# A hybrid encoder layer on one core: another model decides the order of each engine's instructions

## The chip, the core and the metric

The kernel runs on one core of one Trainium2 chip. A core has five engines that each take their own queue of instructions in order: TensorE (PE, with its weight loads shown apart as PEld), VectorE (DVE), ScalarE (ACT), GpSimd (POOL) and SyncE (SP). In this kernel SP issues all transfers between device memory (DRAM) and the on-chip memory (SBUF). Matmul results stand in PSUM, which DVE and ACT read. Engines wait for each other on semaphores. The metric is device time in microseconds (us); each figure is a median of several executions, and one execution more is taken with the profiler.

## The reference

One layer of a bidirectional encoder with parallel head groups, applied with the same weights to two requests: 1024 rows (x_sample) and 256 rows (x_prompt) of width 2048. Each has 256 rows of memory.

```python
hn = rms_norm(x, norm_g)
proj = hn @ w_in
xbc, z_ssd, dt_raw, q, k, v, z_att, mq, z_mem = split_cols(proj, IN_SIZES)
xbc = silu(centred_dwconv(xbc, conv_w, conv_b))           # 5 taps over the rows
y = ssd_scan(forward) + ssd_scan(backward) + d_skip * xs  # chunks of 128 rows, 16 heads
o_ssd = rms_norm(y * silu(z_ssd))                          # two groups of 512
o_att = window_attention(q, k, v, sink) * silu(z_att)      # |t-s| <= 128, 8 heads, 2 kv heads
o_mem = softmax(mq @ mk.T) @ mv * silu(z_mem)              # 4 heads over 256 memory rows
return x + concatenate([o_ssd, o_att, o_mem]) @ w_out
```

All values are float32. q, k, mq and mk are normalised per head.

## The kernel before

The 1280 rows are ten tiles of 128 rows, eight of the sample and two of the prompt, in two row groups of five tiles. A large product with weights is computed in 16 steps over the contraction. Each float32 operand is split into a rounded part (h, or xH) and a rest (l, or xL), and each product is three matmuls: h with xH, l with xH, h with xL (L269 to L271 in `block_tok`, L304 to L306 in `block_feat`). Per step SP loads a weight tile (wraw, L228 or L286), ACT makes wh (L219, or L222 with a gain), DVE makes wl (L220 or L223), and PE multiplies it with all five row tiles. These are the main matmuls. Their results stand in five PSUM banks (acc), which an evacuation function empties.

Beside this main stream runs the side work, written as Python generators that are stepped between the main steps: normalisation statistics, window attention (`attn`, L558), memory attention (`mem_attn`, L665) and the two passes of the SSD scan (`ssd_up`, L757, `ssd_down`, L877). `run` (L942) asks for so many side steps per main step; the rates are written by hand. So the order in which the Python program emits instructions is fixed by hand. It isn't the order on the chip: on leaving the context (L1159), the library's scheduler simulates the machine and picks, for each engine, the next instruction by emission order and by readiness in its simulation; `high_priority` (L253, L273) shifts some of them forward. Buffers are handed out in the same pass, from rings of a fixed size. The queues that result are static: on the chip each engine takes its queue in that order.

The steps of memory attention for one row tile, `mem_attn`, are: SP loads the queries (mq, L669); ACT squares them, DVE sums (mss, L673), POOL makes the reciprocal root (mr, L133 and L134), DVE scales (L677); PE transposes them (pmq, L683); ACT and DVE split them (mqh L685, mql L687); PE makes the scores of two pairs of heads (pms, L699 to L701); DVE takes the maximum (mm, L703), ACT the exponential (mpr, L708), DVE the reciprocal of the sum (mden, L710) and the scaling (L713); PE transposes the probabilities (pmt, L721), ACT copies them (mpT, L723), PE multiplies them with the values (pmo, L734), DVE with the gate (moT, L737); SP stores the transposed result to DRAM (oT, L750).

The output product, four blocks of 512 columns for each row group (`w_out_rows`), takes its stationary operand from four quads xH0 to xH3 (with xL0 to xL3), of which there is one buffer each. While the last block of one group runs, `refill_o` (L975) refills each quad for the other group as soon as the block is past it. Quads 0 and 1 (window and memory attention) are loaded already transposed, by `fill_direct`: load chd (L207), xH on ACT (L210), xL on DVE (L211). Quads 2 and 3 (SSD) are loaded by rows, by `fill_transposed`: load ch (L191), scale on DVE (L193), transpose on PE (pr, L196), xH on ACT (L199), xL on DVE (L200). The evacuation `ev_out` (L392) loads the rows of x (yt, L400), adds the PSUM bank on DVE (L401) and stores (L402). chd, ch and the yt of tiles 0 and 3 share one ring of three buffers (tag "ch", CH in L29).

The context is opened in `kernel`, which the diff touches.

## Time and profile before

| | us |
|---|---|
| median of 3 runs | 1927.21 |
| lowest and highest run | 1923.53 and 1927.83 |
| the profiled execution | 1923.56 |
| its span on the core | 1921.8 |
| PE busy | 1878.3 |
| DVE busy | 1050.8 |
| ACT busy | 763.8 |
| POOL busy | 136.2 |
| mean granted TensorE clock | 0.994 |

The profile's page gives busy time per engine, then the span cut into 40 equal slices with the busy share of each in tenths. Matmuls are pipelined and their ends are modelled, so a busy PE can still be short of its best rate. A row of waits reads: the engine, tile and line that waited, the engine, tile and line that ended the wait, the total in us, how often, the longest. A row of groups reads: line, engine, operation, what it writes and reads, the shape and count, then busy time and the mean of one in ns, then idle time before it and what ended that. A row of the queue of SP or of a timeline reads: start, duration, engine, line, operation. Rows of transfers end with the median time in us from issue to landing. A row of a stretch reads: from and to, length, busy time and count of PE, PEld, DVE, ACT and POOL, the granted clock of TensorE (1 is full), the share of the transfer engines that is busy, and GB/s.

### The profile page before, as it was taken

To read this page: it belongs to the slowest core of one execution; us is meant where nothing else is said; L and a number is where in the kernel's file an instruction comes from. 1 tells how busy PE (TensorE), PEld (TensorE's weight loads), DVE (VectorE), ACT (ScalarE), POOL (GpSimd) and SP (SyncE) were. 2 spreads that over 40 slices of the span, in tenths; PEclk is the share of its full clock that TensorE was granted. 3 is DMA by queue.
4 is the path that set the end of the run, shared out by engine and by line. 5 is a ranking of instruction groups with operands and counts; after the bars stand their busy time and mean duration, and the time that the engine had idled before them with its cause. 6 is when DMAs were issued, how large, how long until landed. Compare 5 with 4: busy or idle time off the path is not lost.

```text
span 1921.8 us, 28750 instructions
## 1 busy us (share of the span) xinstructions
PE 1878.3 (98%) x10568; PEld 1636.4 (85%) x10568; DVE 1050.8 (55%) x2097; ACT 763.8 (40%) x1720; POOL 136.2 (7%) x183
## 2 busy tenths in 40 slices
PE   7999999999999999999999999999999999999999
PEld 6798899998898879899977777988987778878887
DVE  4455327586564554876676555574775554442222
ACT  6556423242442545532325445333633433321111
POOL 0111000000010000100110110100010000000000
PEclk9999999999999999999999999999999999999999
DMA  8766533323443455543435567763465344554442
GB/s 269 264 201 186 165 104 95 107 92 109 122 123 118 159 161 154 155 123 94 118 110 158 147 182 250 233 189 116 151 197 180 118 133 133 179 175 132 134 120 70
DMA packets 191341, 289.42 MB, mean 151 GB/s; under 512 B 18976, under 2 KB 68192, under 8 KB 191200
## 3 DMA queue, kind: packets, MB, share of 16 engines
q1 hardware_dynamic: 191200, 287.58, 48.7%
q8 instruction: 83, 1.36, 0.3%
q14 instruction: 58, 0.48, 0.1%
HBM read 230.59 MB, written 56.92 MB: 150 GB/s over the span
## 4 chain that ended last, share of the span: by engine, by line
PE 80%; DMA 10%; DVE 4%; ACT 4%; issue 2%; POOL 1%; SPq 0%; ACTq 0%; DVEq 0%; POOLq 0%
PE acc L269 14%; PE acc L271 14%; PE acc L270 14%; PE acc L304 9%; PE acc L306 9%; PE acc L305 9%; DMA rf<-ac 2%; PE po L647 1%; DMA rb<-ac 1%; PE py L860 1%; DMA chd<-in_mem_turned_dram 1%; PE ppt L636 1%; PE pmo L734 1%; DMA xst<-in_x_sample_dram 1%; PE psc L606 1%
## 5 line engine op out<-in xcount | busy, mean ns | idle before, releaser
L269 PE MATMUL acc<-wh,xH 128*128 128x512 f32 (+1 forms) x1568 | 619.2, 395 | 15.6 <-ACT wh L219 13.7
L270 PE MATMUL acc<-wl,xH 128*128 128x512 f32 (+1 forms) x1568 | 602.7, 384 | 2.5 <-DVE wl L220 2.5
L271 PE MATMUL acc<-wh,xL 128*128 128x512 f32 (+1 forms) x1568 | 602.6, 384 | 0.0
L220 DVE TENSOR_TENSOR wl<-wraw,wh 128x512 fp32r<-128x512 f32 (+1 forms) x416 | 282.3, 680 | 393.8 <-ACT wh L219 383.7
L219 ACT ACTIVATE wh<-wraw 128x512 fp32r<-128x512 f32 (+1 forms) x416 | 254.4, 613 | 557.8 <-PE acc L271 249.5
L304 PE MATMUL acc<-xH,wh 128*128 128x320 f32 x1280 | 405.9, 317 | 0.4 <-DVE zs L331 0.4
L306 PE MATMUL acc<-xH,wl 128*128 128x320 f32 x1280 | 397.8, 311 | 0.0
L305 PE MATMUL acc<-xL,wh 128*128 128x320 f32 x1280 | 396.3, 310 | 0.0
L269 PEld LDWEIGHTS acc<-wh,xH 128*128 128x128 f32 x1568 | 297.3, 190 | 77.9 <-ACT wh L219 15.2
L270 PEld LDWEIGHTS acc<-wl,xH 128*128 128x128 f32 x1568 | 297.5, 190 | 61.3 <-issue 5.0
L271 PEld LDWEIGHTS acc<-wh,xL 128*128 128x128 f32 x1568 | 297.1, 189 | 57.2 <-issue 1.4
L304 PEld LDWEIGHTS acc<-xH,wh 128*128 128x128 f32 x1280 | 241.1, 188 | 6.4 <-issue 4.9
L305 PEld LDWEIGHTS acc<-xL,wh 128*128 128x128 f32 x1280 | 241.0, 188 | 3.2 <-issue 3.1
L306 PEld LDWEIGHTS acc<-xH,wl 128*128 128x128 f32 x1280 | 240.9, 188 | 0.9 <-issue 0.9
L223 DVE SCALAR_TENSOR_TENSOR wl<-wraw,vec,wh 128x512 fp32r<-128x512 f32 x64 | 48.0, 751 | 120.8 <-ACT wh L222 120.8
L222 ACT ACTIVATE wh<-wraw,vec 128x512 fp32r<-128x512 f32 x64 | 46.3, 724 | 137.5 <-PE acc L271 135.4
L379 DVE SCALAR_TENSOR_TENSOR c<-u,vec,c 128x638 f32<-128x638 f32 (+1 forms) x96 | 84.9, 884 | 1.0
L850 ACT ACTIVATE rb<-rb,wj_all 128x128 f32<-128x128 f32 x160 | 52.2, 390 | 46.6 <-DMA rb<-ac 46.5
L621 ACT ACTIVATE lg<-lg,nm 128x384 f32<-128x384 f32 (+1 forms) x80 | 45.1, 564 | 47.5 <-DVE nm L615 45.5
L850 ACT ACTIVATE rf<-rf,wj_all 128x128 f32<-128x128 f32 x160 | 53.3, 391 | 23.6 <-DMA rf<-ac 23.6
L803 POOL TENSOR_TENSOR ya<-xs,dco 128x512 f32<-128x512 f32 x20 | 29.4, 1479 | 401.7 <-DVE dco L788 259.8
L214 DVE SCALAR_TENSOR_TENSOR xL<-chd,vec,xH 128x640 fp32r<-128x640 f32 (+1 forms) x48 | 40.6, 859 | 29.3 <-ACT xH L213 28.6
(236 smaller groups left out, 1771.5 us busy)
## 6 DMA issues: line engine op xcount, KB each, us to landing
wraw<-in_w_in_laid_dram SPq DMA_DIRECT2D x288, 256.0 KB, 2.8
wraw<-in_w_out_laid_dram SPq DMA_DIRECT2D x128, 256.0 KB, 2.7
chd<-in_x_turned_dram SPq DMA_DIRECT2D x32, 320.0 KB, 3.8
rf<-ac SPq DMA_DIRECT2D x40, 256.0 KB, 3.8
rb<-ac SPq DMA_DIRECT2D x40, 256.0 KB, 4.0
out_dram<-yt SPq DMA_DIRECT2D x40, 256.0 KB, 3.2
wraw<-in_w_mem_laid_dram SPq DMA_DIRECT2D x32, 256.0 KB, 4.9
xst<-in_x_sample_dram SPq DMA_DIRECT2D x32, 256.0 KB, 4.4
```

The costliest lines, as they stand in the source:

```text
L219: A.activation(h, raw, AF.Copy)
L220: V.tensor_sub(l, raw, h.bitcast(F32))
L222: A.activation(h, raw, AF.Copy, scale=g)
L223: V.scalar_tensor_tensor(out=l, in0=raw, scalar=g, in1=h.bitcast(F32), op0=ALU.mult, op1=ALU.subtract)
L269: T.matmul(ps[t][:, :n], sh, h[:, :n], start=(k_ == 0), stop=False)
L270: T.matmul(ps[t][:, :n], sh, l[:, :n], start=False, stop=False)
L271: T.matmul(ps[t][:, :n], sl, h[:, :n], start=False, stop=(k_ == KT - 1))
L304: T.matmul(o, sh, cur["H", q][:, m, c], start=(k == 0), stop=False)
L305: T.matmul(o, sh, cur["L", q][:, m, c], start=False, stop=False)
L306: T.matmul(o, sl, cur["H", q][:, m, c], start=False, stop=(k == KT - 1))
L379: V.scalar_tensor_tensor(out=c[:, :n], in0=u[:, k:k + n], scalar=cw[k], in1=c[:, :n], op0=ALU.mult, op1=ALU.add)
L850: A.activation(r[:, c], r[:, c], AF.Identity, bias=wj_all[:, t, h:h + 1])
```

## The change

One argument of the context is set. With it the scheduler takes the times by which it orders instructions from the library's timeline simulator in place of its default model. The Python program that emits instructions, the tiles, the rings and their sizes, and the stages are unchanged.

```diff
-    with _tile.TileContext(nc) as tc:
+    with _tile.TileContext(nc, schedule_with_timeline_sim=True) as tc:
         hymba_encoder_kernel(tc, *args)
```

Both programs hold the same instructions: 10,020 matmuls, 2,097 on DVE, 1,523 on ACT, 179 on POOL and 1,130 transfers on SP. Set side by side, 4,902 of the matmuls, 1,565 of the DVE instructions, 1,101 of those on ACT, 718 of the transfers and 22 on POOL have another place in their queue. Half of the DVE, ACT and SP instructions move by two places or fewer. On PE the largest move is 294 places. Around the refill of the last output blocks the queue of PE reads as follows after the change (line, tile written and tiles read, shape, count):

```
L269 Matmult acc_17113<-wh_17192,xH0_16731 128x512
...
L683 Matmult pmq_16595<-ident_84,mq_16559 128x128 x4
L699 Matmult pms_16607<-mkH_113,mqh_16600 128x256
...
L721 Matmult pmt_16662<-ident_84,mpr_16617 128x128 x4
L721 Matmult pmt_16669<-ident_84,mpr_16655 128x128 x4
L734 Matmult pmo_16697<-mpT_16667,mv_115 128x128 x4
L734 Matmult pmo_16703<-mpT_16674,mv_115 128x128 x4
L196 Matmult pr_16940<-ident_84,ch_16937 128x128 x4
L196 Matmult pr_16950<-ident_84,ch_16947 128x128 x4
L196 Matmult pr_16981<-ident_84,ch_16978 128x128 x4
L196 Matmult pr_16991<-ident_84,ch_16988 128x128 x4
L196 Matmult pr_17022<-ident_84,ch_17019 128x128 x4
L269 Matmult acc_17116<-wh_17120,xH0_16731 128x512
```

In the queue before, 30 main matmuls stand between pmq_16595 and the last pmo_16703, and 225 between that and the last refill transpose, pr_17183; after the change these are 0 and 48.

## The prediction

> **What bounds the kernel now.** I read the page's busy table, its slices and chain, then the waits of PE over the whole span and by stretch, then the stretch from 1600 us. TensorE is the bound: PE is busy in every slice, and the chain is 80% PE.

> ```profile
> span 1921.8 us, 28750 instructions
> PE 1878.3 (98%) x10568; PEld 1636.4 (85%) x10568; DVE 1050.8 (55%) x2097; ACT 763.8 (40%) x1720; POOL 136.2 (7%) x183
> PE   7999999999999999999999999999999999999999
> PE 80%; DMA 10%; DVE 4%; ACT 4%; issue 2%; POOL 1%; SPq 0%; ACTq 0%; DVEq 0%; POOLq 0%
> ```

> So only two things can change: how long PE waits, and at what clock it runs. The matmuls are the same, with the same shapes. The waits of PE, whole span (all rows sum to some 39 us, of which 7.9 is the wait before the first matmul):

> ```profile
> PE acc L269 <- ACT wh L219: 13.7, 4, 7.9
> PE psc L606 <- ACT pT L637: 3.7, 3, 1.8
> PE pr L196 <- DVE ch L193: 3.4, 4, 1.6
> PE pyb L903 <- DVE state L912: 3.0, 1, 3.0
> PE acc L270 <- DVE wl L220: 2.5, 5, 1.4
> PE py L860 <- DVE rb L853: 2.3, 3, 1.3
> ```

> Cut by stretch, the waits sum to 10 us from the first matmul to 210 us, 19.5 us in 23 waits between 210 and 1600, and one wait of 1.6 us after 1600. The last matters most: between 1600 and 1720 the kernel finishes the last attention tiles of the second row group and refills the stationary operand for the last four output blocks, and PE loses 1.6 us over it. The queue shows why: the loads that refill are spread over 50 us, beside main matmuls.

> ```profile
> 1626.49 1.06 SPq L669 DMA_DIRECT2D mq<-mq  x1
> 1650.09 0.94 SPq L750 DMA_DIRECT2D oT<-moT  x1
> 1655.79 1.06 SPq L207 DMA_DIRECT2D chd<-oT  x2
> 1669.45 1.06 SPq L191 DMA_DIRECT2D ch<-o  x2
> 1699.97 0.36 SPq L191 DMA_DIRECT2D ch<-o  x1
> ```

> (mq starts the last memory-attention tile, oT stores its result, chd and ch are refill loads.) The profiled execution took 1923.56 us: 1921.8 of span and 1.8 around it. It equals the fastest of the three runs (1923.53) and is 3.65 under their median; my sum is made against 1923.56.

> **The change part by part.** No instruction is added or removed; every engine's queue is re-sorted. I place each PE instruction of the new order at the sum of the time that the instructions ahead of it took on PE in the profile.

> *Side work sinks behind the main matmuls.* In the new order attention, SSD and memory attention stand later, the main matmuls earlier. The query transposes pmq (L683) of the five memory-attention tiles of the second group move later by 21, 36, 48, 60 and 58 us of PE work. The main matmuls ahead of them cost the same 0.227 us, so this is free until main matmuls run out. They run out at the last tile: between its first transpose and its last pmo matmul (L734) stood 30 main matmuls, now none; between its first transpose and the eighth of the ten refill transposes pr (L196) stood 240, which are 54 us, now 23, which are 5.2 us. PE takes its queue in order, so behind pmq it can do nothing else.

> *What the chain there needs.* SP has the same inversion: the load of mq (L669), formerly 18 rows ahead of oT's store, now stands 3 ahead of it, and then come all four chd loads, five ch loads, two yt loads, one more ch load, two stores and two ch loads, with no weight load between. chd, ch and two of five yt tiles share one ring of three buffers (CH, L29). Durations are means or medians of the profile's groups:

> ```profile
> mq<-mq SPq DMA_DIRECT2D x10, 256.0 KB, 3.6
> oT<-moT SPq DMA_DIRECT2D x10, 256.0 KB, 3.3
> chd<-oT SPq DMA_DIRECT2D x16, 320.0 KB, 3.7
> ch<-o SPq DMA_DIRECT2D x20, 256.0 KB, 3.2
> yt<-in_x_sample_dram SPq DMA_DIRECT2D x32, 256.0 KB, 4.4
> out_dram<-yt SPq DMA_DIRECT2D x40, 256.0 KB, 3.2
> ```

> 1. mq load 3.6, square 0.63, sum 0.69, rsqrt on POOL 0.19 and 1.01, scaling 0.69, with hand-overs: 6.9 us.
> 2. pmq to the last pmo: transposes 0.6, split 0.58 and 0.68, twelve pms 1.4, maximum 0.69 and 0.17, two exp with their accumulator reads 1.3, reciprocal 0.17, two scalings 0.7, pmt 0.6, copy 0.59, pmo 1.8: 9 us.
> 3. Two moT products 0.8, store 3.3, chd load 3.7, split 0.73 and 0.82, which together with one more split (0.8) frees a ring buffer; ch load 3.2, scaling 0.48: 13.8 us.
> 4. pr 0.3; the third ch load waits for the fourth chd, itself late in the ring: 3.0; two more pr and their scalings 0.6: 3.9 us.
> 5. yt load into the buffer that a pr frees, 4.4, and the addition (L401) 0.69, without which PE's next main matmul has no PSUM bank: 5.1 us.
> 6. yt store 3.2, ch load 3.2, scaling 0.48, a little queueing, and behind it on DVE the wl split 0.69 of the next weights: 7.9 us.

> That is 46.6 us. PE has work in it: 2.3 us between mq's issue and pmq, 23 main matmuls 5.2, and side matmuls (4 pmq, 12 pms, 8 pmt, 8 pmo, 32 pr) 8.0: 15.5 us. PE waits 46.6 - 15.5 = 31.1 us. With the slower landings that such loads also had here (the chain lists a ch load of 4.80 us) it is 37.5; with the quick ones (some 2.6 us for a ch load) 27. I take 34, between median and slow. The old wait of 1.6 goes.

> *The clock.* After PE's wait of 2.44 us before 199.2, its granted clock was 0.50 for 5.4 us, and matmuls stood 0.43 us apart instead of 0.227:

> ```profile
> 199.20:204.60 5.40, 5.38 (x12) 4.02 (x13) 1.38 (x2) 3.79 (x9) 0.00 (x0) 0.50 0.38 120
> ```

> The new chain has waits of about 4, 14, 4, 4 and 2.5 us, so its own matmuls run at half clock (pms, pmt and pmo on the path: +2.6), and the first 12 main matmuls behind it (12 x 0.2 = 2.4): +5. Bounds: 0 if the clock stays up, 8 if all 13 us of PE work doubled and lay half on the path. [...]

> *The waits elsewhere.* All 23 waits between 210 and 1600 stand at side matmuls or evacuations that the new order puts later, each by more PE work than it waited (the 3.0 at pyb by 6.8 us, the 1.8 at psc by 4.8). But their inputs come from ACT and DVE queues that were re-sorted too, and steps that wait for each other still follow each other (pyf behind the cb copy, pst behind xf). Bounds: 0 and -19.5; I take -8, nearer to none than to all, as a wait put later often comes back one step on. Before 210 us the transfers are the limit (DMA share 0.71, against 0.47 after), and only the order of splits changes: 0 to -10, I take -3. With those go one or two slow-clock stretches: -1. Together -12.

> Sum: 1923.6 - 1.6 + 34 + 5 - 12 = 1949.

> **The rivals.** (a) *Nothing comes back elsewhere*: the waits removed are replaced, one for one. For it: ACT and DVE carry the same chains. Against: PE has more main work ahead of every old wait. Time: 1949 + 12 = 1961, up to 1966 with slow landings. (b) *The order pays elsewhere and ends faster*: all 29.5 us of old waits go, with 4 to 5 us of low clock, -34 in all, and the refill chain costs less than that. For it: 23 of 23 places have more cover. It decides for faster from a refill below 34 us with its clock, that is, ch and chd loads at their quick 2.6 us while the weight loads are out of their way: 1923.6 - 1.6 + 27 + 2 - 34 = 1917. Against: these loads took up to 4.8 us here. (c) *The refill chain is cheap but the rest goes as I forecast*: 1923.6 - 1.6 + 27 + 2 - 15 = 1936. (d) *The new order says nothing on the chip, because waits decide the sequence anyway*: 1924; against it, queues are taken in order, and 217 main matmuls have left the gap.

> **How the numbers follow.** Forecast 0.68 (1938 to 1960: refill 31 to 38, clock 2 to 7, elsewhere -17 to -8), (a) 0.15, (c) 0.10, (b) 0.05, (d) 0.02. A measurement of this kernel tells 0.2% (3.9 us) from no change. Slower by more: forecast, (a) and (c), 0.93. The range reaches to (c) and most of (a): 1934 to 1965.

> **What would show it.** PE idle 30 to 38 us in one cluster near 1680 to 1740, at pmq, pmt, pr and L269, the largest a pr that waits 13 to 16 us for L193; ch and chd landings packed into 35 us with hardly a weight load; granted clock near 0.5 there; PE waits between 210 and 1600 near 11 us. Wrong if the pr wait is under 8 us, or if main matmuls wait for wh or wl all along, which the same order could bring if ACT is late.

## The result, and the profile after

| | before | after |
|---|---|---|
| median of 4 runs, us | 1926.41 | 1946.60 |
| lowest and highest run | 1923.53 and 1927.83 | 1945.28 and 1951.25 |
| the profiled execution | 1923.56 | 1947.09 |
| its span | 1921.8 | 1945.4 |

The changed kernel takes 1.0112 times as long, 95% interval 1.0095 to 1.0128. The forecast was 1949, range 1934 to 1965. The page of the profile after, its first lines, the slices of PE and of its clock, and the shares of the chain:

```profile
span 1945.4 us, 28765 instructions
PE 1880.3 (97%) x10568; PEld 1639.4 (84%) x10568; DVE 1049.7 (54%) x2097; ACT 761.6 (39%) x1720; POOL 136.3 (7%) x183
...
PE   7999999999999999999999999999999999869999
...
PEclk9999999999999999999999999999999999879999
...
PE 77%; DMA 14%; ACT 3%; DVE 3%; issue 1%; SPq 1%; POOL 0%; POOLq 0%; ACTq 0%; DVEq 0%
```

PE is busy 2.0 us longer and idle 21.6 us longer (span less busy: 43.5, now 65.1). Where before every slice but the first read 9, the two from 1653 to 1751 us now read 8 and 6, and the granted clock dips to 8 and 7 tenths in the same two. The waits of PE from 1680 to 1740 us in the kernel after (us in total, times, longest):

```profile
PE pr L196 <- DVE ch L193: 16.8, 3, 12.2
PE pmq L683 <- DVE mq L677: 3.7, 1, 3.7
PE pmt L721 <- DVE mpr L713: 1.9, 1, 1.9
PE acc L269 <- DVE yt L401: 1.8, 1, 1.8
PE pms L699 <- ACT mqh L685: 0.7, 1, 0.7
```

These are 24.9 us where the kernel before lost 1.6. They are waits of the chain that the prediction walked, sorted here by size; in time, pmq comes first, then pms, pmt, pr, the acc that waits for yt, and a last pr. The queue of SP after, from mq on (start, duration, engine, line, operation):

```profile
1683.26 0.33 SPq L400 DMA_DIRECT2D yt<-in_x_prompt_dram  x1
1683.64 0.42 SPq L669 DMA_DIRECT2D mq<-mq  x1
...
1702.40 0.51 SPq L750 DMA_DIRECT2D oT<-moT  x1
1705.01 4.94 SPq L207 DMA_DIRECT2D chd<-oT  x4
1710.41 6.31 SPq L191 DMA_DIRECT2D ch<-o  x5
1719.24 1.33 SPq L400 DMA_DIRECT2D yt<-in_x_sample_dram  x2
1721.15 0.33 SPq L191 DMA_DIRECT2D ch<-o  x1
...
1727.17 0.89 SPq L191 DMA_DIRECT2D ch<-o  x2
1731.69 0.33 SPq L228 DMA_DIRECT2D wraw<-in_w_out_laid_dram  x1
```

No weight load is issued between 1684 and 1731. The loads of oT and o, which before lay over 50 us beside main matmuls, follow each other here, and no main matmul runs between 1686.9 and 1722.9. The chain that ended last passes through the same steps (start, duration, piece):

```profile
1683.64 3.41 DMA mq<-mq
...
1699.30 2.62 PE pmo L734 x16
...
1702.40 2.54 DMA oT<-moT
...
1705.40 3.38 DMA chd<-oT
...
1710.41 3.01 DMA ch<-o
...
1719.24 2.82 DMA yt<-in_x_sample_dram
...
1722.87 4.24 DMA out_dram<-yt
1727.17 2.60 DMA ch<-o
...
1730.49 0.63 PE pr L196 x4
```

Not all of the loss is waiting. I take the time from the start of each PE instruction to the start of the next, without the waits, and subtract the median of its kind (same line and shape; these medians add up to 1851 us in both programs). Between 1600 and 1760 us this excess is 1.6 us before and 9.7 after, and it grows where the granted clock is low: 8.4 of the 9.7 belong to matmuls that started while it was 0.50. So the refill costs 23.3 us of waits and 8.1 of slow matmuls, 31.4 together. The whole span grew by 23.6: the rest of the kernel became 7.8 us shorter. 6.2 of these lie between 180 and 210 us (waits and excess: 7.3 before, 1.1 after), 1.6 in all the rest. That last figure is a balance of larger ones, and two traces of the changed kernel show how far one trace carries: from 210 to 1600 us its waits and excess are 32.7 us here and 20.8 in x11 below, with 33.3 before.

### The profile page after: what moved, and what is told of

The parts are those of the page before. It is cut to its first block, busy times and chain, and to the rows that moved or that the text cites. A ratio compares the mean times of both kernels' runs of the same rounds, so it can differ in the third digit from the quotient of the medians.

```text
span 1945.4 us, 28765 instructions
## 1 busy us (share of the span) xinstructions
PE 1880.3 (97%) x10568; PEld 1639.4 (84%) x10568; DVE 1049.7 (54%) x2097; ACT 761.6 (39%) x1720; POOL 136.3 (7%) x183
## 4 chain that ended last, share of the span: by engine, by line
PE 77%; DMA 14%; ACT 3%; DVE 3%; issue 1%; SPq 1%; POOL 0%; POOLq 0%; ACTq 0%; DVEq 0%
PE acc L270 13%; PE acc L269 13%; PE acc L271 13%; PE acc L304 9%; PE acc L306 9%; PE acc L305 9%; DMA rb<-ac 2%; DMA rf<-ac 2%; DMA xst<-in_x_sample_dram 2%; PE po L647 2%; PE ppt L636 1%; PE py L860 1%; DMA chd<-in_mem_turned_dram 1%; ACT rf L850 1%; PE pmo L734 1%
## 5 line engine op out<-in xcount | busy, mean ns | idle before, releaser
L270 PE MATMUL acc<-wl,xH 128*128 128x512 f32 (+1 forms) x1568 | 602.0, 385 | 3.9 <-DVE wl L220 3.8
L269 PE MATMUL acc<-wh,xH 128*128 128x512 f32 (+1 forms) x1568 | 584.1, 392 | 19.2 <-ACT wh L219 16.4
L220 DVE TENSOR_TENSOR wl<-wraw,wh 128x512 fp32r<-128x512 f32 (+1 forms) x416 | 284.7, 688 | 338.1 <-ACT wh L219 329.1
L219 ACT ACTIVATE wh<-wraw 128x512 fp32r<-128x512 f32 (+1 forms) x416 | 253.5, 612 | 491.0 <-PE acc L271 213.4
L304 PE MATMUL acc<-xH,wh 128*128 128x320 f32 x1280 | 401.4, 314 | 0.8 <-ACT qs L340 0.6
L269 PEld LDWEIGHTS acc<-wh,xH 128*128 128x128 f32 x1568 | 293.5, 189 | 82.6 <-ACT wh L219 20.2
L270 PEld LDWEIGHTS acc<-wl,xH 128*128 128x128 f32 x1568 | 296.2, 189 | 63.2 <-DVE wl L220 6.5
L851 DVE COPY_PREDICATED rb<-upper,rf 128x512 f32<-128x512 uint32 x40 | 31.5, 788 | 70.2 <-ACT rb L850 62.5
## 6 DMA issues: line engine op xcount, KB each, us to landing
wraw<-in_w_in_laid_dram SPq DMA_DIRECT2D x288, 256.0 KB, 2.8
wraw<-in_w_out_laid_dram SPq DMA_DIRECT2D x128, 256.0 KB, 2.7
rf<-ac SPq DMA_DIRECT2D x40, 256.0 KB, 3.5
rb<-ac SPq DMA_DIRECT2D x40, 256.0 KB, 4.8
out_dram<-yt SPq DMA_DIRECT2D x40, 256.0 KB, 2.7
wraw<-in_w_mem_laid_dram SPq DMA_DIRECT2D x32, 256.0 KB, 4.9
xst<-in_x_sample_dram SPq DMA_DIRECT2D x32, 256.0 KB, 4.5
```

The costliest lines, as they stand in the source:

```text
L219: A.activation(h, raw, AF.Copy)
L220: V.tensor_sub(l, raw, h.bitcast(F32))
L269: T.matmul(ps[t][:, :n], sh, h[:, :n], start=(k_ == 0), stop=False)
L270: T.matmul(ps[t][:, :n], sh, l[:, :n], start=False, stop=False)
L304: T.matmul(o, sh, cur["H", q][:, m, c], start=(k == 0), stop=False)
```

## The experiments

Each group of runs had its own runs of the kernel before beside it (medians 1926.4 for the result, 1922.0 for x1 to x4, 1921.3 for x5 to x8, 1919.9 for x9 to x11), so I compare ratios. "Refill" is the stretch from 1600 to 1760 us.

| run | ratio to before, 95% interval | waits at the refill | excess there | lost 180 to 210 |
|---|---|---|---|---|
| before | 1 | 1.6 | 1.6 | 7.3 |
| after | 1.0112 (1.0095 to 1.0128) | 24.9 | 9.7 | 1.1 |
| x1 default order, 'o' 1.6 | 1.0117 (1.0099 to 1.0135) | 19.6 | 9.7 | 8.1 |
| x2 default order, 'o' 2.0 | 1.0032 (1.0015 to 1.0048) | 7.7 | 6.0 | 6.8 |
| x3 new order, early attention | 0.9960 (0.9946 to 0.9975) | 1.3 | 0.7 | 0.7 |
| x4 new order, no round trip | 1.0035 (1.0023 to 1.0047) | 11.1 | 7.8 | 1.0 |
| x5 early block, default | 1.0093 (1.0078 to 1.0108) | 1.4 | 2.2 | 2.4 |
| x6 early block, timeline | 1.0088 (1.0071 to 1.0105) | 1.4 | 2.3 | 0.1 |
| x7 new order, memory last | 1.0050 (1.0032 to 1.0068) | 12.9 | 11.4 | 1.0 |
| x8 x3 and x7 together | 0.9966 (0.9952 to 0.9980) | 1.1 | 1.1 | 0.2 |
| x9 default order, early attention | 0.9982 (0.9969 to 0.9994) | 0.8 | 0.5 | 6.5 |
| x10 as x3 | 0.9966 (0.9952 to 0.9980) | 0.7 | 0.5 | 1.5 |
| x11 after again | 1.0080 (1.0059 to 1.0101) | 21.9 | 9.4 | 0.1 |

### x1 and x2: the same loss under the default order

My theory is that the loss is one place, the refill that no main matmul covers, because memory attention ends too late. The rival is that the simulator's order costs a little everywhere. If the theory is right, the default order must lose the same when memory attention is made late by hand, and lose in steps with the cover.

```diff
-          'o': 2.6})
+          'o': 1.6})
```

> The kernel before (default model), with one number changed: the side steps asked for per main step of the output blocks fall from 2.6 to 1.6 (RATES 'o'). That alone puts the memory attention of the second row group as late as the new order put it: in the queue of PE 7,611 main matmuls stand ahead of the last pmo and of the first five refill transposes, as in the changed kernel (before: 7,389 and 7,524 to 7,554). Theory (the loss is the refill that no main matmul covers): the same group of waits appears, a pr wait of 11 to 15 us for L193 first, 20 to 27 us of PE waits in all near 1690 to 1735, and some 8 us of slow matmuls beside them; 1926 + 23 + 6 = 1955 us, between 1945 and 1962. Rival (the simulator's order costs it, by many places all over): the default order is kept, so 1926 us, within 5.

The other run has 2.0 in that place.

> The same edit by half: 'o' from 2.6 to 2.0. 7,519 main matmuls stand ahead of the last pmo, 92 fewer than in the changed kernel, and 7,575 to 7,591 ahead of the first five refill transposes. Theory: 92 main matmuls are 21 us of cover, about what the chain from the last pmo to the last pr needs beyond its own work, so most of the loss is not there yet: 1927 to 1937 us, best guess 1932 (waits of 1 to 3 us at two or three refill transposes). Rival: 1926 us.

Measured: x1 1943.97 beside 1921.98, x2 1928.58. PE's waits of x1 from 1600 to 1760 us:

```profile
PE pr L196 <- DVE ch L193: 14.9, 5, 12.5
PE pmq L683 <- issue: 3.1, 3, 1.4
PE acc L269 <- DVE yt L401: 0.9, 1, 0.9
PE pmt L721 <- DVE mpr L713: 0.7, 2, 0.5
```

and of x2:

```profile
PE pmq L683 <- issue: 4.7, 3, 2.2
PE pr L196 <- DVE ch L193: 2.7, 4, 1.0
PE acc L269 <- DVE yt L401: 0.3, 1, 0.3
```

The default order, with one rate lowered, waits at four of the same five places, with much the same longest wait (12.5, against 12.2), and loses 22 us. The rival's 1926 is out. With 92 main matmuls (21 us) of cover the long pr wait is gone, and 6 to 7 us are lost, as expected. In size x1 is a miss: I expected 29 us more than before, and it was 22 (1943.97 is just under the range of 1945 to 1962; the kernel before ran 4 us faster beside it than in the result). The waits came to 19.6 us, under the 20 to 27 expected. By the two traces waits and excess at the refill grew by 26.1 us, so the rest of the gap lies outside it, where single traces of one kernel differ by as much.

### x3: the new order with the cover restored

```diff
-... 'mq': 2.75, 'zm': 2.54,
+... 'mq': 4.0, 'zm': 5.2,
```

> The changed kernel (timeline simulator), with two numbers changed: the side steps asked for beside the blocks mq and zm of the second row group rise from 2.75 and 2.54 to 4.0 and 5.2. Window attention of that group ends earlier, memory attention starts earlier, and 7,473 main matmuls stand ahead of the last pmo in place of 7,611, 7,541 ahead of the first refill transpose. Theory: of the 24.9 us of waits at the refill some 3 stay, and the slow clock there goes (8 us): 1946.6 - 22 - 8 = 1917 us, with about 4 us of new waits at the earlier window attention 1921; range 1914 to 1930. Rival (the order costs everywhere): nothing of this touches the rest, 1940 to 1947 us.

Measured: 1914.32 beside 1921.98. All waits of PE from 1600 to 1760 us in x3:

```profile
PE pr L196 <- DVE ch L193: 1.3, 2, 1.1
```

The order of the simulator stays, the refill is covered, and the kernel is now faster than both others. So the order itself costs nothing on balance; what it does to one place does (what the two rates do by themselves is x9's question). The rival (1940 to 1947) is out.

### x4: what part the round trip through oT has

```diff
-                return [part(fill_direct, q, j, oT_d[q][grp][:, j, :]) for j in range(4)]
+                return [part(fill_direct, q, j, oT_d[q][0][:, j, :]) for j in range(4)]
```

> The changed kernel, but the last refill of the quad of memory attention reads oT of the first row group, which has long been stored, in place of the second group's (so the memory part of the last five row tiles is left out of the output product). All transfers, matmuls and the order of PE at the refill stay; only the wait of the four chd loads for the last oT store goes. Theory (the chain pmo, store of oT, chd, ch, pr is what PE waits for): the 12.2 us wait at pr falls below 3, PE waits near the refill 5 to 8 us in place of 24.9, and 1946.6 - 18 - 4 = 1924 us, range 1919 to 1931. Rival (the ring of three buffers and the packed transfers are the limit, whatever oT does): the pr wait stays above 8 us, 1938 us or more.

Measured: 1929.30 beside 1921.98, with the memory part of the last five row tiles left out of the output. PE's waits of x4 from 1600 to 1760 us, but for one of 0.7:

```profile
PE pr L196 <- DVE ch L193: 5.5, 3, 2.4
PE pmq L683 <- issue: 3.0, 1, 3.0
PE pmt L721 <- DVE mpr L713: 1.9, 1, 1.9
```

The 12.2 is gone, as the theory says; the rival's 8 us or more at pr isn't there. By the ratios (1.0112 to 1.0035) some 15 us go, where I had expected 22: of the waits 11.1 stay, not 5 to 8, and of the excess 7.8 of 9.7, not half. The several waits of 1 to 3 us that are left go with a low clock as well: 0.50 from 1686 to 1696 and from 1703 to 1709, with PE 73% and 86% busy.

### x7 and x8: the memory quad last

```diff
-            need((attn, mem_attn, ssd_down, ssd_down)[q], range(grp * 5, grp * 5 + 5))
-            if q < 2:
-                return [part(fill_direct, q, j, oT_d[q][grp][:, j, :]) for j in range(4)]
+            need((attn, ssd_down, ssd_down, mem_attn)[q], range(grp * 5, grp * 5 + 5))
+            if q in (0, 3):
+                return [part(fill_direct, q, j, oT_d[q // 3][grp][:, j, :]) for j in range(4)]
...
-    inputs['w_out_laid'] = _np.concatenate([att, w[1536:], w[:1024]]) ...
+    inputs['w_out_laid'] = _np.concatenate([att, w[:1024], w[1536:]]) ...
```

> The changed kernel with the order of the quads in the output product changed: window attention, SSD, SSD, memory attention, in place of attention, memory, SSD, SSD (the rows of w_out are laid out to match). Memory attention's quad is then refilled last and needed last, 180 main matmuls (41 us) into the next block. The lateness of memory attention itself stays: 7,611 main matmuls stand ahead of its last pmo. Theory (the long wait is the round trip through oT standing ahead of the refill transposes in the queues): pmq and pmt still wait 3.7 and 1.9 us, the 12.2 at pr falls to waits of 2 to 3 each; some 11 us of waits in place of 24.9 and half of the slow matmuls: 18 us under the changed kernel, 4 us over the kernel before (1926 beside 1922; range 1920 to 1932). Rival (packed loads and the ring of three set the refill's pace, whatever comes first): no less than 14 us over the kernel before.

> The timeline simulator's order with both repairs: the side rates beside mq and zm of the second row group at 4.0 and 5.2, and the memory quad last. Theory: no wait at the refill (1.3 with the rates alone), a 3.5 us wait of a transpose of the window attention gone; so 2 to 3 us under the version with the rates alone, 10 us under the kernel before (1912 beside 1922; range 1908 to 1917). Rival: the refill has no more to give, 1914 within 2.

Measured: x7 1931.55 beside 1921.34, x8 1914.68. x7 takes the long wait away with nothing left out of the computation (the waits at pr are now five, 6.1 us in all, 2.5 the longest), so it was the round trip standing ahead of the refill transposes. But it is 10 us over the kernel before, where I had said 4: the excess didn't halve, it was 11.4. x8 gives nothing over x3: where the refill is covered, the order of the quads has no more to save, which is what its rival said.

### x5 and x6: the early part alone, without a verdict

The new order's own gain lies near 200 us. To test it alone, the part up to `gate_att(0)` is put into a block with its own order (the body moves in by four columns; later x_stats loads no longer wait for a load in the block).

```diff
+    with tc.block(schedule_with_timeline_sim=True):
+        vec = const([P, R_N], "vec")
...
+        gate_att(0)
+    last_load[0] = None
     queue(0, attn, range(4))
```

The control has `tc.block()`.

> A control for the next one. The kernel before, with everything up to the end of gate_att(0) (the first 240 us or so) put into a block of its own, ordered by the default model. The boundary costs something by itself, because no load crosses it: worked from the rows of before, one wait of some 22 us at the first matmul behind it. So 1922 + 22 = 1944 us, between 1936 and 1956. The place at 195 to 205 us stays as in the kernel before: an L269 that waits 2.4 to 2.8 us for wh and matmuls at half clock behind it, some 7 us lost in waits and slow matmuls between 180 and 210 us.

> The same block, ordered by the timeline simulator; everything behind it is ordered by the default model, as in the control. Theory (of the 9 us that the new order gains away from the refill, 6 come from this one place near 200 us, where the default order puts a weight load behind two loads of x rows that wait for a buffer): 6 us under the control, the 2.4 us wait and the half clock gone, about 1 us lost between 180 and 210 us. Rival (the gain is spread over the waits between 210 and 1600 us, as I had forecast): within 2 us of the control.

Measured: x5 1940.14, x6 1940.86, beside 1921.34. The boundary costs a wait of 22.7 and of 23.0 us, as expected. But the control didn't keep the place that it was to keep: it lost only 2.4 us between 180 and 210 us. The block changed the default order there too: no rf or rb stands in ACT's queue between 186 and 206 us. So the pair can't tell what the place is worth, and my 6 us between the two were not seen. No gain of the simulator's order before 180 us is to be seen either (waits and excess 14.4 us in the control, 16.3 in x6; the two traces of the changed kernel have 13.9 and 17.4).

My reason in that expectation (a weight load behind two loads of x rows) doesn't hold either. The queue of ACT in the kernel before (start, duration, engine, line, operation, idle before):

```profile
193.21 0.63 ACT L925 ACTIVATE xst<-xst 128x512 f32<-128x512 f32 x1 [1.35 <-DMA xst<-in_x_sample_dram]
...
193.84 0.39 ACT L850 ACTIVATE rf<-rf,wj_all 128x128 f32<-128x128 f32 x1
194.13 0.61 ACT L852 ACTIVATE rb<-rb 128x512 f32<-128x512 f32 x1
194.65 0.61 ACT L219 ACTIVATE wh<-wraw 128x512 fp32r<-128x512 f32 x1
...
198.55 0.61 ACT L219 ACTIVATE wh<-wraw 128x512 fp32r<-128x512 f32 x1
```

and in the kernel after:

```profile
191.59 0.62 ACT L219 ACTIVATE wh<-wraw 128x512 fp32r<-128x512 f32 x1
...
194.96 0.61 ACT L219 ACTIVATE wh<-wraw 128x512 fp32r<-128x512 f32 x1
```

wh stands behind an xst that waits 1.35 us for its load, and behind other side work (rf, rb); the next wh, at 198.55, is the one that PE waits 2.44 us for. Its own load had been issued at 191.44 and had landed 3.1 us later. After the change the first of the two stands ahead of that xst, and they run 3.1 and 3.6 us earlier. In the four executions of the default order without a block (before, x1, x2, x9) 6.5 to 8.1 us are lost between 180 and 210 us, in the seven of the new order (after, x3, x4, x7, x8, x10, x11) 0.1 to 1.5. The place is real and goes with the order; that the order of ACT is its cause is read from the two queues and wasn't isolated by a run.

### x9, x10 and x11: order and rates, two by two

> The kernel before (default model) with the two rates of the repaired kernel, 4.0 beside mq and 5.2 beside zm of the second row group. In the queue of PE its refill transposes stay where they were (7,524 to 7,554 main matmuls ahead of the first five), its last pmo comes earlier (7,029 ahead). Theory (with the refill covered, what the new order has over the default order is the place near 200 us, not the rates): no change, 0 to -2 us of the kernel before, with the 7 us between 180 and 210 us still lost. Rival (the rates are what beats the kernel before, under either order): 6 to 8 us under the kernel before.

> The same rates under the timeline simulator once more, beside the other three on one chip: 7 to 8 us under the kernel before (0.996), PE waits at the refill 1 to 2 us, about 1 us lost between 180 and 210 us.

> The changed kernel itself beside them: 1.0095 to 1.0128 times the kernel before as measured, so 18 to 25 us over it, and 26 to 33 us over the version with the two rates, of which the refill is all.

Measured beside 1919.92: x9 1916.01, x10 1913.34, x11 1934.29. The rates help the default order too, by 0.2% (0.06 to 0.31%), more than my theory's 0 to 2 us would have it and less than its rival's 6 to 8. Under the new order they gain 21 us, to 6.6 under the kernel before (7 to 8 expected). x11's 14 us over the kernel before are fewer than the 18 to 25 that I took from the first measurement (the two intervals, 1.0095 to 1.0128 and 1.0059 to 1.0101, just overlap). I had also said that the refill is all of the difference to x10. The refill differs by 30 us (31.3 against 1.2), but x10 loses 7.8 us more than x11 between 1200 and 1600 us (waits and excess 9.9 against 2.1), where it packs the window attention. The other traces bear this out: 9.8 to 10.0 us there in x3, x8 and x10, 1.9 to 4.9 in after, x4, x7 and x11. The waits there of x10:

```profile
PE ppt L636 <- DVE lg L626: 3.5, 1, 3.5
```

So cover that is moved to one place is taken from another, and 21 of 30 us are kept. The kernel of x3 and x10 is the fastest measured here and beats both the kernel before and the changed one. It also beats x9, though the two intervals against the kernel before overlap: the twelve runs of each, taken side by side, have means 3.0 us apart, with a 95% interval of 0.9 to 5.1 (worked out from their scatter). So with the refill covered the new order is worth some 3 us by itself.

## Why the prediction was right, and which terms were off

The direction, the place and the mechanism held. Time 1946.6 against 1949. Step by step:

1. **Main matmuls run out at the last memory-attention tile.** Right: shown by the rows above, by x1 (lateness alone makes the loss, under the default order) and by x3 (with the cover back it is gone).
2. **The chain's length.** I added 46.6 us from the issue of mq on; the last pr that PE waited for started 46.8 us after it (1683.64 to 1730.49). Within it, mq to pmq took 7.0 (6.9 forecast), pmq to the last pmo 11.3 (9 and 2.6 for the clock), that to the first pr 12.2 (13.8). The yt load took 2.8 us where I had put 4.4, and the slower pr made up for it.
3. **The size of the waits: 34, taken between median and slow landings.** Too large: 24.9. No load came near the slow landings: the store of oT took 2.5 us against 3.3, the chd loads 2.9 to 3.8 against 3.7, the ch loads 2.6 to 3.3 against 3.2. No weight load was among them, but the share of the transfer engines was 0.55 from 1704 to 1731, against 0.64 from 1660 to 1712 before, and why they landed sooner isn't shown. By medians alone the step had given 31.1. The rest of the gap is the clock: from 1683.64 to 1730.49 PE's own instructions took 21.9 us, not 15.5, and 7.6 of them are excess, 7.0 of that at a granted 0.50. Slow side matmuls stand inside the chain, where PE would else have waited, so part of a wait became busy time.
4. **The clock, +5.** Too small: the excess grew by 8.1. I had let the clock recover about 5 us after each wait; it stayed low through most of the short matmuls (10.8 of 13.8 us of PE's work, below). Steps 3 and 4 together: 34 - 1.6 + 5 = 37.4 forecast, 31.4 measured.
5. **Waits between 210 and 1600 us, -8.** Too much: 19.5 before, 18.6 after. The places I named did shrink (psc 3.7 to 1.2, pyb by state 3.0 to none), and others came in their stead. PE's waits from 210 to 1600 us after, the largest rows:

```profile
PE pyf L812 <- ACT cb L779: 5.3, 2, 3.1
PE acc L269 <- ACT wh L219: 3.6, 3, 2.0
PE pxs L794 <- ACT cb L779: 1.7, 1, 1.7
```

   By this trace rival (a), replaced one for one, was right for this stretch, but one trace is too little: x11, the same kernel, has 11.7. Over the four traces of the new order with the old rates (after, x4, x7, x11) these waits are 11.7 to 18.6 us, 15.8 in the mean; over the three of the default order (before, x1, x2) 19.0 to 20.7, 19.7 in the mean. So some 4 us went, about half of the 8. With the excess added, 20.8 to 32.7 against 25.9 to 33.3, the two orders can't be told apart there.
6. **Before 210 us -3, slow clock elsewhere -1.** Too small: 6.2 us went in the one place near 200 us, 2.6 of them waits and 3.6 the matmuls behind these. Before, the granted clock was 0.50 from 199.2 to 204.6; after, it was 1.00 from 196 to 206. So the one wait of before cost more than twice its length.
7. **The sum.** The refill was forecast 6.0 too dear and the rest (-12 against -7.8) 4.2 too generous; the two partly cancel, which is why 1949 was so near. That part was luck. So was the base: as a change the forecast was +25.4 us, from a profiled run at the fast end, and the medians moved by 20.2 in the result and by 14.4 in x11. And rival (c) was added up with -15 for the rest, where the forecast has -12; with that it is 1939, which changes no reading here.

Of the signs named, the cluster, the packed loads, the clock near 0.5 and the largest wait at pr were seen; the wait was 12.2, not 13 to 16, the cluster 24.9, not 30 to 38, and the waits from 210 to 1600 fell to 11 in x11's trace alone.

## What to carry to other kernels

A new order of the same instructions is to be judged by where the main work runs out before the side work does: count the main matmuls ahead of each late chain in the queue, and compare their time with the chain's. A wait that an order removes need not be a gain: other waits came in place of some of those removed; here such waits went from some 20 us to some 16, while one uncovered chain cost 31. When an order is bad in one place, repair the place (here two rates) before giving up the order.

## What the runs showed of the hardware

```profile
1686.00:1690.00 4.00, 0.91 (x8) 0.60 (x6) 1.53 (x4) 0.63 (x1) 1.20 (x2) 1.00 0.46 138
1690.00:1700.00 10.00, 6.71 (x28) 5.65 (x29) 4.45 (x12) 3.72 (x11) 0.00 (x0) 0.52 0.05 14
1700.00:1704.00 4.00, 1.92 (x14) 1.72 (x13) 0.85 (x2) 0.00 (x0) 0.00 (x0) 0.91 0.10 29
1704.00:1720.00 16.00, 4.05 (x16) 2.87 (x16) 6.81 (x12) 4.74 (x7) 0.00 (x0) 0.50 0.54 173
1720.00:1722.00 2.00, 1.12 (x5) 0.71 (x4) 1.25 (x2) 1.19 (x2) 0.00 (x0) 0.71 0.73 169
1722.00:1730.00 8.00, 4.82 (x22) 3.80 (x22) 2.61 (x5) 2.38 (x4) 0.00 (x0) 1.00 0.57 189
1732.00:1734.00 2.00, 2.00 (x9) 1.60 (x8) 2.00 (x4) 0.23 (x1) 0.00 (x0) 0.50 0.62 165
```

During the idle time before 1690 the clock is still granted in full (1.00 from 1686 to 1690). It is at half for 10 us (0.52) while PE is 67% busy with pmq, pms and pmt, and comes back within 1700 to 1702 (0.83 there, 1.00 from 1702 to 1704), after pmt and pmo had run without a pause from 1697.3. Then it is at half for 16 us more (0.50), through 10 us in which PE waits and through the first pr, and comes back within 1720 to 1722 (0.71 there, 1.00 from 1722 to 1730), after twelve pr had run without a pause from 1718.1. After the yt wait of 1.8 us the main matmuls at 1722.9 ran at full speed (1.00, 0.23 us apart); the wait of 2.77 us that ended at 1730.49 was followed by half clock from 1732 on (0.50 until 1734), after PE had taken up work. So for this chain of short matmuls with waits between them most of it was paid at half clock: of PE's 13.8 us between 1690 and 1722, 10.8 lie in the two rows at 0.52 and 0.50. Long waits were not needed for that: in x4 and x7, where no wait at the refill was longer than 3.1 us, the excess was 7.8 and 11.4 us (in x7 the granted clock was 0.50 from 1704 to 1720, with PE busy for 11.4 of the 16 us).
